# First feed-forward product by Strassen blocks, and the second half of w_out by tokens, in one layer of a hybrid trunk

## The chip, the cores and the metric

One core of a Trainium2 chip. The metric is the device time of one execution in microseconds (us), the median of a few runs. TensorE is called PE, VectorE DVE, ScalarE ACT, GpSimd POOL and SyncE SP; in the code they are `PE` (and `mm` for its matmul), `V`, `S`, `G`, and `dma` is a load that SP issues.

## The reference, cut to what matters

One layer over 640 tokens of 1024 channels: 128 context tokens and 512 latent tokens, which have modulations of their own (shift, scale and gate out of the conditioning). Three mixers work side by side on parts of the channels; then come their output product and a feed-forward net, all in float32.

```python
def trunk_layer(x, mod, ...):
    shift1, scale1, gate1, shift2, scale2, gate2 = jnp.split(mod, 6, axis=-1)
    ...
    mixed = jnp.concatenate([y_a, y_b, y_c], axis=-1)     # 512 + 256 + 256 channels
    x = x + gate1 * jnp.einsum('blc,cd->bld', mixed, w_out)        # 1024 x 1024
    h = rms_norm(x, norm2_g) * (1 + scale2) + shift2
    ff = jnp.square(jax.nn.relu(jnp.einsum('bld,df->blf', h, w_ff1)))   # 1024 x 4096
    x = x + gate2 * jnp.einsum('blf,fd->bld', ff, w_ff2)           # 4096 x 1024
    return x, s_fin
```

A last norm (`final_norm_g`) follows the layer.

## The kernel before

Activations lie channel-major: 128 channels on the partitions, the 640 tokens along the free axis. A float32 product is made of three passes: each operand is split into a high part (`whi`, `fh`, `mh`, made by an ACT cast to fp32r) and a rest (`wlo`, `fl`, `ml`, made by a subtraction on POOL for weights and on DVE for activations), and PE adds high·high, high·rest and rest·high into one bank of PSUM. The 640 tokens are two halves of 320 columns, so that a block of 128 output channels takes 6 matmuls for each 128 input channels. `pm()` hands out the 8 banks of PSUM in turn, all of them named `pb`.

Weights come as 128x512 pieces (`raw`, 256 KB, 2 places) that `wsplit` turns into `whi` and `wlo` (3 places, `WB`). Every engine issues its instructions in a fixed order, written out ahead by a scheduler; an instruction that waits holds up all behind it on its engine.

The mixers and the first half of `w_out` (`out_half`, channels of the FNet and pooling mixers) run in one scheduled stretch that ends at 644.64 us. What follows is what the change touches:

- the second half of `w_out`: the RWKV mixer's output comes back from DRAM (`ycd`, tiles `yc2`), is split into `mh2` and `ml2`, and 8 blocks of 48 matmuls are added, gated, to `x1`. Behind each block ACT and DVE make `h2h` and `h2l`, the parts of `x1` times norm gain and scale but without the norm's division; ACT squares `x1` and POOL adds the squares up (`ssq`).
- the second norm: sums over channels by matmuls with `ones`, mean and epsilon (`st2`) on DVE, the power -0.5 on POOL, a copy along the columns (`rsb`) on DVE, transposes on PE and a copy on ACT give `rs`, the reciprocal root of each token. PE is meanwhile given the first two blocks of the next product (`ahead`), since that uses the operands that are not yet divided.
- the feed-forward net in four quarters of 1024 hidden channels: 8 blocks of the first product (`w_ff1`, 8 x 6 matmuls each; the second half has 2 columns more, which carry the shift), then 8 of the second (`w_ff2`). Behind a block of the first, DVE multiplies by `rs`, ACT adds the shift and takes relu, DVE squares, ACT and DVE split (`fh`, `fl`).
- the last quarter of `w_ff2` runs over 384 tokens and then over 256, with the final norm behind it.

## Time and profile before

| | |
|---|---|
| median of 3 runs (lowest, highest) | 1137.36 us (1137.35, 1138.07) |
| profiled execution | 1140.2 us, which is its span too: nothing of it lies outside |
| PE busy | 1095.3 us (96%) |
| DVE, ACT, POOL busy | 544.5, 506.4, 383.3 us |
| PE's granted clock, mean | 0.983 of full speed |
| chain that ended last | PE 82%, issue 6%, DVE 6%, POOL 2%, ACT 1% |

The three runs lie within 0.07% of each other, and the profiled execution is 2.8 us longer than their median. Times inside the kernel below are from its start. A matmul's busy time is longer than the distance to the next one, since they overlap; what a matmul costs is the distance between starts.

### The profile page before, as it was taken

What the parts mean: (1) busy time and instruction counts of PE and PEld (TensorE: products, weight loads), DVE (VectorE), ACT (ScalarE), POOL (GpSimd) and SP (SyncE); (2) the same over time, 40 slices, a digit from 0 to 9 for tenths busy, and PEclk for the clock granted to TensorE, in tenths of its full rate; (3) what the DMA queues carried; (4) which work ended last, traced back from release to release, by engine and by line L of the source; (5) the groups of instructions that cost most, each with busy time, mean ns of one, the idle gap of its engine ahead of it and who ended that gap; (6) DMA issues with size and microseconds to landing.
All of it is one profiled execution on the core that took longest, in us unless ns stands there. A gap on an engine that the chain in (4) does not pass through costs nothing.

```text
span 1140.2 us, 23679 instructions
## 1 busy us (share of the span) xinstructions
PE 1095.3 (96%) x9516; PEld 949.0 (83%) x9516; DVE 544.5 (48%) x1297; ACT 506.4 (44%) x1221; POOL 383.3 (34%) x462
## 2 busy tenths in 40 slices
PE   5999999999999998998999999999999999999996
PEld 3688888788785665565677999999999999999996
DVE  6266665466665654667754664311331233123313
ACT  5243575655565454654762354312431243124412
POOL 4224431124222133464300283333333333333520
PEclk9999999999998999998999999999999999999999
DMA  9522311111313345442313322222222222222212
GB/s 321 184 62 81 94 36 58 51 51 43 95 64 121 112 139 166 124 133 69 111 56 97 117 74 75 75 75 75 75 76 80 76 76 75 75 74 75 77 45 93
DMA packets 130383, 104.11 MB, mean 91 GB/s; under 512 B 9309, under 2 KB 108642, under 8 KB 130274
## 3 DMA queue, kind: packets, MB, share of 16 engines
q1 hardware_dynamic: 114290, 81.22, 23.5%
q10 hardware_dynamic: 15552, 21.05, 6.2%
q8 instruction: 75, 1.23, 0.4%
q0 software_dynamic: 432, 0.33, 0.2%
q14 instruction: 34, 0.28, 0.1%
HBM read 90.52 MB, written 9.76 MB: 88 GB/s over the span
## 4 chain that ended last, share of the span: by engine, by line
PE 82%; issue 6%; DVE 6%; POOL 2%; ACT 1%; DMA 0%; ACTq 0%; DVEq 0%; POOLq 0%
PE pb L248 82%; DVE t L248 1%; DVE EB L248 1%; DVE bda L248 1%; POOL st L248 1%; DVE P L248 1%; DVE hlo L248 0%; DVE BK L248 0%; POOL t L248 0%; DMA wpl<-w_pool 0%; POOL bda L248 0%; ACTq L248 0%; DVE dd L248 0%; DVE W L248 0%; DVE y L248 0%
## 5 line engine op out<-in xcount | busy, mean ns | idle before, releaser
L248 POOL TENSOR_TENSOR wlo<-raw,whi 128x512 fp32r<-128x512 f32 x125 | 162.3, 1299 | 268.5 <-ACT whi L248 266.2
L248 ACT CAST whi<-raw 128x512 fp32r<-128x512 f32 x161 | 99.8, 620 | 276.6 <-PE pb L248 251.0
L248 PE MATMUL pb<-h2l,whi 128*128 128x320 f32 (+1 forms) x512 | 155.4, 310 | 0.0
L248 PE MATMUL pb<-h2h,whi 128*128 128x320 f32 (+1 forms) x512 | 155.3, 311 | 0.0
L248 DVE SCALAR_TENSOR_TENSOR x<-pb,mod,x 128x128 f32<-128x128 f32 (+1 forms) x144 | 55.0, 433 | 172.9 <-PE pb L248 172.7
L248 PE MATMUL pb<-fh,whi 128*128 128x320 f32 (+2 forms) x408 | 123.3, 310 | 0.0
L248 PE MATMUL pb<-fl,whi 128*128 128x320 f32 (+2 forms) x408 | 122.7, 308 | 0.0
L248 PE MATMUL pb<-h2h,wlo 128*128 128x320 f32 (+1 forms) x512 | 117.0, 310 | 0.0
L248 PE MATMUL pb<-hhi,whi 128*128 128x320 f32 (+1 forms) x304 | 99.1, 331 | 0.0
L248 PE MATMUL pb<-hlo,whi 128*128 128x320 f32 (+1 forms) x304 | 98.6, 329 | 0.4 <-DVE hlo L248 0.4
L248 PEld LDWEIGHTS pb<-h2l,whi 128*128 128x128 f32 x512 | 96.6, 189 | 0.0
L248 PEld LDWEIGHTS pb<-h2h,whi 128*128 128x128 f32 x512 | 96.5, 189 | 0.0
L248 PE MATMUL pb<-fh,wlo 128*128 128x320 f32 (+2 forms) x408 | 94.6, 309 | 0.0
L248 PEld LDWEIGHTS pb<-h2h,wlo 128*128 128x128 f32 x512 | 86.3, 188 | 0.0
L248 POOL TENSOR_TENSOR t<-t,k 128x256 f32<-128x256 f32 (+1 forms) x24 | 15.9, 664 | 208.2 <-DVE t L248 197.5
L248 PE MATMUL pb<-hhi,wlo 128*128 128x320 f32 (+1 forms) x304 | 78.8, 328 | 0.0
L248 PEld LDWEIGHTS pb<-fh,whi 128*128 128x128 f32 x408 | 77.1, 189 | 0.0
L248 PEld LDWEIGHTS pb<-fl,whi 128*128 128x128 f32 x408 | 76.3, 187 | 0.0
L248 DVE TENSOR_TENSOR rl<-pb,rs 128x320 f32<-128x320 f32 x64 | 30.3, 486 | 94.3 <-PE pb L248 94.1
L248 PEld LDWEIGHTS <-bda 128*128 128x128 f16 x880 | 43.1, 99 | 37.8 <-issue 13.9
L248 ACT COPY W<-pb 128x256 f32<-128x256 f32 (+3 forms) x144 | 54.4, 398 | 41.5 <-DVE W L248 29.2
L248 PEld LDWEIGHTS pb<-fh,wlo 128*128 128x128 f32 x408 | 68.6, 188 | 0.0
(271 smaller groups left out, 2399.7 us busy)
## 6 DMA issues: line engine op xcount, KB each, us to landing
raw<-w_ff SPq DMA_DIRECT2D x128, 256.0 KB, 2.8
wa<-w_ada SPq DMA_DIRECT2D x64, 256.0 KB, 3.2
wa<-w_ada SPq DMA_DIRECT2D x16, 512.0 KB, 8.7
raw<-w_in SPq DMA_DIRECT2D x30, 256.0 KB, 2.9
raw<-w_out SPq DMA_DIRECT2D x16, 256.0 KB, 2.8
ukd<-shq ACTq DMA_DIRECT2D x9, 320.0 KB, 2.5
ds<-dft_s ACTq DMA_DIRECT2D x8, 257.0 KB, 2.7
x<-x_sample SPq DMA_DIRECT2D x4, 512.0 KB, 5.8
```

Source lines behind the costliest of these rows:

```text
L248: return fn(out, *a, **k)
```

## The change

The first feed-forward product is done by the Strassen-Winograd scheme on 2 x 2 blocks: two neighbouring blocks of 128 hidden channels (a pair, 16 in all), two halves of the input channels, and two halves of the tokens. Seven products of 4 x 3 matmuls of 320 columns take the place of eight. Four of the seven use sums of weight pieces (`sw`, made on DVE from `rw`, the raw weights of a pair as two loads of 512 KB), and five use sums of activation blocks (`t1` to `t4`, split into `T1` to `T4`; `B11`, `B21`, `B22` are plain blocks). The sums across token halves need operands that are already normalized, so the norm's division, scale and shift are applied to `x1` first (`h2`), and the two extra columns and the multiplication by `rs` behind the product are gone. The products are added up by 7 DVE additions a pair; relu and square are one DVE instruction on 320 columns, followed by the split as before, also on 320.

The second half of `w_out` runs over the first 384 tokens, all 8 blocks, then over the last 256, and each part has sums, root and transposes of its own behind it. The products `w11` and `w12` of the first `LEAD` = 3 pairs need the first half of the tokens alone and are put ahead of the other operands. The place of the final norm's gain and of the first four pieces of the last quarter's weights moves to the end of the feed-forward net.

```diff
-        h2h = fc.tile([P, KB, NT + 2], F32R, name="h2h")
-        h2l = fc.tile([P, KB, NT + 2], F32R, name="h2l")
-        rs = fc.tile([P, NT], F32, name="rs")
+        ba = fc.tile([P, 4 * QW], F32R, name="ba")
+        h2 = fc.tile([P, KB, NT], F32, tag="fh", name="h2")
+        spare = fc.tile([P, KB, NT], F32, tag="fl", name="spare")
...
+        fw = es3.enter_context(tc.tile_pool(name="fw", bufs=1))
+        TOK = ((0, 384), (384, NT))
...
+                r.append(fw.tile([P, 4, 2, P], F32, tag="rw", name="rw", bufs=3))
+                dma(r[-1][:], src[:, 4 * k:4 * k + 4, c0:c0 + 2 * P].rearrange("p k (f c) -> p k f c", f=2))
...
+        def split(w):
+            hi = fw.tile([P, 4, P], F32R, tag="fhi", name="fhi", bufs=6)
+            lo = fw.tile([P, 4, P], F32R, tag="flo", name="flo", bufs=6)
+            S.copy(hi[:], w)
+            G.tensor_tensor(lo[:], w, hi[:].bitcast(F32), op=ALU.subtract)
+            return hi, lo
...
+        def product(w, x):
+            ps = pm()
+            n = 0
+            for kb in range(4):
+                for a, b in ((w[0], x[0]), (w[0], x[1]), (w[1], x[0])):
+                    mm(ps[:, 0:HB], a[:, kb, :], b[:, kb, :], start=n == 0, stop=n == 11)
+                    n += 1
+            return ps[:, 0:HB]
...
+        def lead(w11, w12):
+            p1 = new()
+            S.copy(p1[:], product(w11, B11))
+            c = new()
+            V.tensor_tensor(c[:], p1[:], product(w12, B21), op=ALU.add)
+            return p1, c
...
+                s = fw.tile([P, 4, P], F32, tag="sw", name="sw", bufs=3)
+                V.tensor_tensor(s[:], x, y, op=op)
...
+            s1 = ws(a[1][0], a[1][1], ALU.add)
+            s2 = ws(s1, a[0][0], ALU.subtract)
+            w6 = split(s2)
+            w7 = split(ws(a[0][0], a[1][0], ALU.subtract))
+            w5 = split(s1)
+            w3 = split(ws(a[0][1], s2, ALU.subtract))
+            w4 = split(a[1][1])
...
+            V.tensor_tensor(u2[:], p1[:], product(w6, T2), op=ALU.add)
+            V.tensor_tensor(u3[:], u2[:], product(w7, T3), op=ALU.add)
+            p5 = product(w5, T1)
+            V.tensor_tensor(c22[:], u3[:], p5, op=ALU.add)
+            V.tensor_tensor(u2[:], u2[:], p5, op=ALU.add)
+            emit(1, 1, c22)
+            V.tensor_tensor(u2[:], u2[:], product(w3, B22), op=ALU.add)
+            emit(0, 1, u2)
+            V.tensor_tensor(u3[:], u3[:], product(w4, T4), op=ALU.subtract)
+            emit(1, 0, u3)
...
+                V.scalar_tensor_tensor(c[:], c[:], 0.0, c[:], op0=ALU.max, op1=ALU.mult)
+                last[0] = S.copy(fh[:, b, HALF[h]], c[:]).ins
+                V.tensor_tensor(fl[:, b, HALF[h]], c[:], fh[:, b, HALF[h]].bitcast(F32), op=ALU.subtract)
...
-        with tc.tile_pool(name="mo", bufs=1) as mo:
+        with tc.tile_pool(name="mo", bufs=1, side="right") as mo:
...
+            wo = []
+            for i, (lo, hi) in enumerate(TOK):
+                n = hi - lo
+                for b in range(KB):
+                    if i == 0:
+                        r = wp.tile([P, 4, P], F32, tag="raw", name="raw", bufs=RB)
+                        dma(r[:], w_out[:, 0:4, b * P:(b + 1) * P])
+                        wo.append(wsplit(None, 0, 0, G, r) if b < WB else split(r[:]))
+                    w = wo[b]
...
+                            mm(ps[:, 0:n], x[:, kb, :], y[:, kb, lo:hi], start=m == 0, stop=m == 11)
...
+                        sq = sqs[:, b % 2, :]
+                        S.activation(sq[:, 0:n], x1[:, b, lo:hi], AF.Square)
+                        G.tensor_tensor(ssq[:, lo:hi], ssq[:, lo:hi], sq[:, 0:n], op=ALU.add)
...
+                V.tensor_scalar(st[:, 0:nt], ps[:, 0:nt], 1.0 / D, 1e-6, op0=ALU.mult, op1=ALU.add)
+                G.tensor_tensor(st[:, 3:3 + nt], st[:, 0:nt], half[:, 0:nt], op=ALU.pow)
+                V.tensor_copy(A[:, 0:nt, :], st[:, 3:3 + nt].unsqueeze(2).broadcast_to([P, nt, P]))
...
+                    PE.transpose(ps[:, k * P:(k + 1) * P], A[:, k, :], ident[:])
+                S.copy(rs[:, lo:hi], ps[:, 0:n])
+                cs = HALF[i]
+                for b in range(KB):
+                    V.tensor_tensor(h2[:, b, cs], x1[:, b, cs], rs[:, cs], op=ALU.mult)
+                    for k, ss in ((0, slice(0, NP_)), (1, slice(NP_, HB))) if i == 0 else ((1, cs),):
+                        S.activation(h2[:, b, ss], h2[:, b, ss], AF.Identity, scale=gs2[:, b, k:k + 1], bias=mod[:, 24 + b, k:k + 1])
+                if i == 0:
+                    for k, x in enumerate((B11, B21)):
+                        S.copy(x[0], h2[:, 4 * k:4 * k + 4, cs])
+                        V.tensor_tensor(x[1], h2[:, 4 * k:4 * k + 4, cs], x[0].bitcast(F32), op=ALU.subtract)
...
+        for p in range(LEAD):
+            w11, w12 = wsplit(w_ff1, 2 * p * P, 0, G), wsplit(w_ff1, 2 * p * P, 1, G)
+            first_pairs.append(lead(w11, w12))
...
+        def operand(x, v, eng):
+            S.copy(x[0], v)
+            eng.tensor_tensor(x[1], v, x[0].bitcast(F32), op=ALU.subtract)
+        V.tensor_tensor(t1, b12, b11, op=ALU.subtract)
+        V.tensor_tensor(t2, b22, t1, op=ALU.subtract)
+        operand(T2, t2, V)
+        V.tensor_tensor(t3, b22, b12, op=ALU.subtract)
+        operand(T3, t3, V)
+        operand(T1, t1, G)
+        V.tensor_tensor(t4, t2, b21, op=ALU.subtract)
+        operand(B22, b22, V)
+        operand(T4, t4, V)
...
+        for q in range(4):
+            for p in range(4 * q, 4 * q + 4):
+                r = raw2(w_ff1, 2 * p * P)
+                if p >= LEAD:
+                    first_pairs.append(lead(split(r[0][:, :, 0, :]), split(r[1][:, :, 0, :])))
+                p1, c = first_pairs.pop(0)
+                squares(p)(0, 0, c)
+                rest(p1, r, squares(p))
...
-                pss = gemm(w_out, b * P, (mh, ml), G, (0,))
-                xb = x1[:, b, :]
+                pss = gemm(w_ff2[q], b * P, (fh, fl), G)
                 for h in range(2):
-                    gated(xb, pss[h], h, 2, b, xb)
-                for i, cs in SEG:
-                    S.activation(h2h[:, b, cs], xb[:, cs], AF.Copy, scale=gs2[:, b, i:i + 1])
-                    V.scalar_tensor_tensor(h2l[:, b, cs], xb[:, cs], gs2[:, b, i:i + 1], h2h[:, b, cs].bitcast(F32), op0=ALU.mult, op1=ALU.subtract)
...
-            ahead = [gemm(w_ff1, 0, (h2h, h2l), G, extra=2)]
...
-            ahead.append(gemm(w_ff1, P, (h2h, h2l), G, extra=2))
...
-                    pss = ahead.pop(0) if ahead else gemm(w_ff1, (q * KB + b) * P, (h2h, h2l), G, extra=2)
-                    sb = ffp.tile([P, 2], F32, tag="sb", name="sb", bufs=3)
-                    V.tensor_copy(sb[:], pss[1][:, HB:HB + 2])
...
-                        V.tensor_tensor(t[:, HALF[h]], pss[h][:, 0:HB], rs[:, HALF[h]], op=ALU.mult)
-                    for i, cs in SEG:
-                        S.activation(t[:, cs], t[:, cs], AF.Relu, bias=sb[:, i:i + 1])
-                    V.tensor_tensor(t[:], t[:], t[:], op=ALU.mult)
-                    last = S.copy(fh[:, b, :], t[:]).ins
-                    V.tensor_tensor(fl[:, b, :], t[:], fh[:, b, :].bitcast(F32), op=ALU.subtract)
```

Three places of the static order, before and now. The names are those of the diff; the number behind a name is the tile's.

SP's queue where the RWKV output is loaded back (`yc2`); `raw` are pieces of `w_out` in the second half and the last of the first half. Before:

```order
L248 DMA raw_9330<-w_out 128x4x128 [waits DMAHW3_49,DVE_49]
L248 DMA raw_9427<-w_out 128x4x128 [waits DMAHW4_49,DVE_49]
L248 DMA yc2_9408<-ycd0_157 128x640 [waits DMAHW3_49,DMAHW5_49,PE_49,Pool_49]
L248 DMA yc2_9412<-ycd1_158 128x640 [waits DMAHW6_49]
L248 DMA yc2_9416<-ycd2_159 128x640 [waits DMAHW7_49]
L248 DMA yc2_9420<-ycd3_160 128x640 [waits DMAHW0_49]
L248 DMA raw_9467<-w_out 128x4x128 [waits DMAHW1_49,DMAHW2_49,DVE_49,Activation_49]
```

Now:

```order
L249 DMA raw_9425<-w_out 128x4x128 [waits DMAHW7_49,DMAHW4_49,DVE_49]
L249 DMA rw_9950<-w_ff1 128x4x256 [waits DMAHW6_49,PE_49,Pool_49]
...
L249 DMA raw_9447<-w_out 128x4x128 [waits DMAHW5_49,DVE_49]
L249 DMA raw_9470<-w_out 128x4x128 [waits DMAHW7_49,Pool_49]
L249 DMA rw_10068<-w_ff1 128x4x256
L249 DMA raw_9493<-w_out 128x4x128 [waits DMAHW2_49,Pool_49]
L249 DMA yc2_9409<-ycd0_157 128x640 [waits PE_49]
L249 DMA yc2_9413<-ycd1_158 128x640
L249 DMA yc2_9417<-ycd2_159 128x640 [waits DMAHW0_49]
L249 DMA yc2_9421<-ycd3_160 128x640 [waits DMAHW1_49]
L249 DMA raw_9516<-w_out 128x4x128 [waits DMAHW3_49,Pool_49]
```

Ahead of the four loads of `yc2` now stand three loads of `rw` and three of `raw`; the last two of `raw` wait for POOL.

PE from the second half of `w_out` to the first feed-forward product; `ident` marks the transposes. Before (`mh` and `h2h` are the products around them):

```order
L248 MATMUL pb<-mh_9406,wlo 128x320 x2
L248 MATMUL pb<-h2h,whi 128x320 [waits DMASW0_49,DMASW2_49,DVE_49,Activation_49]
...
L248 MATMUL pb<-h2h,wlo 128x322
L248 MATMUL pb<-ones,ssq 128x1 [waits PE_49,Pool_49]
L248 MATMUL pb<-ones,ssq 128x1 x4
L248 MATMUL pb<-h2h,whi 128x320
...
L248 MATMUL pb<-h2h,wlo 128x322
L248 MATMUL pb<-ident,rsb 128x128 [waits DVE_49]
L248 MATMUL pb<-ident,rsb 128x128 x3
...
L248 MATMUL pb<-h2h,whi 128x320 [waits Activation_49]
```

Now (`spare` holds the sums of squares and the spread-out root, `ba` is `B11` and `B21`):

```order
L249 MATMUL pb<-mh_9407,flo 128x384
L249 MATMUL pb<-ones,spare 128x1 [waits DMASW0_49,DVE_49,DMASW2_49,PE_49,Pool_49]
L249 MATMUL pb<-ones,spare 128x1 x2
L249 MATMUL pb<-ident,spare 128x128 [waits DVE_49,PE_49]
L249 MATMUL pb<-ident,spare 128x128 x2
L249 MATMUL pb<-mh_9407,whi 128x256 [waits PE_49]
...
L249 MATMUL pb<-mh_9407,flo 128x256
L249 MATMUL pb<-ones,spare 128x1 [waits DVE_49,Pool_49]
L249 MATMUL pb<-ones,spare 128x1
L249 MATMUL pb<-ident,spare 128x128 [waits DVE_49]
L249 MATMUL pb<-ident,spare 128x128
L249 MATMUL pb<-ba,whi 128x320 [waits Activation_49]
```

Before, `ones` and the transposes each had a block of `h2h` products ahead of them; now both stand directly behind the products of `w_out` whose tokens they belong to, and the products with 256 columns, or with `ba`, behind them.

POOL around the root of the norm (`st2`, `halfm`): `ssq` and `spare` are the sums of squares, `wlo` and `flo` weight splits. Before:

```order
L248 TENSOR_TENSOR wlo_9794<-raw_9791,whi_9793 128x512 [waits DMAHW1_49,PE_49,Activation_49]
L248 TENSOR_TENSOR ssq_9424<-ssq_9424,sq_9714 128x640 [waits Activation_49,Pool_49]
L248 TENSOR_TENSOR wlo_9835<-raw_9832,whi_9834 128x512 [waits DMAHW2_49,PE_49,Activation_49]
L248 TENSOR_TENSOR ssq_9424<-ssq_9424,sq_9756 128x640 [waits Activation_49,Pool_49]
L248 TENSOR_TENSOR wlo_9865<-raw_9862,whi_9864 128x512 [waits DMAHW3_49,PE_49,Activation_49]
L248 TENSOR_TENSOR st2_9827<-st2_9827,halfm_87 128x5 [waits DVE_49]
L248 TENSOR_TENSOR wlo_9934<-raw_9931,whi_9933 128x512 [waits DMAHW4_49,PE_49,Activation_49]
```

Now, for the last 256 tokens:

```order
L249 TENSOR_TENSOR spare_9398<-spare_9398 128x256 [waits Activation_49]
L249 TENSOR_TENSOR spare_9398<-spare_9398 128x256 [waits Activation_49,Pool_49]
L249 TENSOR_TENSOR wlo_9811<-raw_9808,whi_9810 128x512 [waits DMAHW7_49,PE_49,Activation_49]
L249 TENSOR_TENSOR spare_9398<-spare_9398 128x256 [waits Activation_49,Pool_49] x2
L249 TENSOR_TENSOR wlo_9817<-raw_9814,whi_9816 128x512 [waits DMAHW0_49,PE_49,Activation_49]
L249 TENSOR_TENSOR spare_9398<-spare_9398 128x256 [waits Activation_49,Pool_49] x2
L249 TENSOR_TENSOR flo_9968<-sw_9965,fhi_9967 128x512 [waits PE_49,Activation_49]
L249 TENSOR_TENSOR spare_9398<-spare_9398 128x256 [waits Activation_49,Pool_49]
L249 TENSOR_TENSOR flo_9972<-sw_9957,fhi_9971 128x512 [waits PE_49,Activation_49]
L249 TENSOR_TENSOR st2_9779<-st2_9779,halfm_87 128x2 [waits DVE_49]
```

Seven additions of 256 columns stand there, with four splits of the first pair's weights among them and the root behind.

## Rows read from the trace of the kernel before

**Rows 1.** The page's first lines: span, and busy time of each engine.

```profile
span 1140.2 us, 23679 instructions
...
PE 1095.3 (96%) x9516; PEld 949.0 (83%) x9516; DVE 544.5 (48%) x1297; ACT 506.4 (44%) x1221; POOL 383.3 (34%) x462
```

**Rows 2.** The chain that ended last, in order of time: start us, us, what.

```profile
628.13 503.34 PE pb L248 x3414
```

**Rows 3.** Windows: us, busy us (count) of PE, PEld, DVE, ACT, POOL; PEclk; DMA.

```profile
900.00:1000.00 100.00, 100.00 (x680) 100.00 (x680) 27.67 (x59) 32.33 (x53) 36.18 (x28) 1.00 0.26 75
```

**Rows 4.** Groups by form, 700 to 1040 us: count, busy us, mean ns.

```profile
L248 POOL TENSOR_TENSOR wlo<-raw,whi 128x512 fp32r<-128x512 f32 x97 | 125.3, 1292 | 217.8 <-ACT whi L248 217.8
...
L248 DVE TENSOR_TENSOR rl<-pb,rs 128x320 f32<-128x320 f32 x48 | 22.9, 486 | 79.1 <-PE pb L248 79.1
L248 DVE TENSOR_TENSOR fl<-rl,fh 128x640 fp32r<-128x640 f32 x25 | 20.6, 826 | 19.8 <-ACT fh L248 19.8
...
L248 ACT ACTIVATE rl<-rl,sb 128x512 f32<-128x512 f32 x24 | 17.4, 725 | 0.0
L248 DVE SCALAR_TENSOR_TENSOR x<-pb,mod,x 128x320 f32<-128x320 f32 x24 | 13.0, 542 | 0.0
...
L248 ACT ACTIVATE rl<-rl,sb 128x128 f32<-128x128 f32 x24 | 9.7, 404 | 1.8
```

**Rows 5.** The window of the second half of w_out, columns as in rows 3.

```profile
644.64:672.80 28.16, 28.16 (x194) 28.16 (x193) 22.64 (x40) 17.87 (x32) 21.87 (x15) 1.00 0.27 77
```

**Rows 6.** Timeline of PE in the tail: start us, us, instruction.

```profile
1076.06 0.34 PE L248 MATMUL pb<-fh,whi 128*128 128x384 f32 x1
...
1076.58 0.34 PE L248 MATMUL pb<-fh,h2h 128*128 128x384 f32 x1
...
1118.27 0.28 PE L248 MATMUL pb<-fh,h2l 128*128 128x256 f32 x1
...
1118.63 0.28 PE L248 MATMUL pb<-fh,h2l 128*128 128x256 f32 x1
```

**Rows 7.** Timeline of SP's queue.

```profile
624.32 12.17 SPq L248 DMA_DIRECT2D raw<-w_out  x2
636.65 2.81 SPq L248 DMA_DIRECT2D yc<-ycd  x4
```

**Rows 8.** Timeline of ACT.

```profile
640.65 0.73 ACT L248 CAST mh<-yc 128x640 fp32r<-128x640 f32 x1 [0.56 <-DMA yc<-ycd]
...
644.54 0.73 ACT L248 CAST mh<-yc 128x640 fp32r<-128x640 f32 x1 [0.16 <-DMA yc<-ycd]
```

**Rows 9.** Timeline of DVE.

```profile
681.14 0.17 DVE L248 TENSOR_SCALAR st<-pb 128x5 f32<-128x5 f32 x1 [5.17 <-PE pb L248]
682.59 0.82 DVE L248 COPY rsb<-st 128x640 f32<-128x640 f32 x1 [1.29 <-POOL st L248]
...
693.88 1.53 DVE L248 TENSOR_TENSOR fl<-rl,fh 128x640 fp32r<-128x640 f32 x1 [0.31 <-ACT fh L248]
```

**Rows 10.** Timeline of POOL.

```profile
655.68 1.57 POOL L248 TENSOR_TENSOR ssq<-ssq,sq 128x640 f32<-128x640 f32 x1 [1.26 <-ACT sq L248]
...
658.52 2.03 POOL L248 TENSOR_TENSOR ssq<-ssq,sq 128x640 f32<-128x640 f32 x1
...
681.38 1.18 POOL L248 TENSOR_TENSOR st<-st,halfm 128x5 f32<-128x5 f32 x1 [2.74 <-DVE st L248]
...
693.30 1.43 POOL L248 TENSOR_TENSOR wlo<-raw,whi 128x512 fp32r<-128x512 f32 x1 [3.19 <-ACT whi L248]
```

**Rows 11.** Group by form on DVE, 644 to 682 us.

```profile
L248 DVE SCALAR_TENSOR_TENSOR h2l<-x,gs,h2h 128x512 fp32r<-128x512 f32 x8 | 8.6, 1076 | 1.6 <-ACT h2h L248 1.6
```

**Rows 12.** Windows before the second half of w_out, columns as in rows 3.

```profile
626.00:631.00 5.00, 3.06 (x9) 2.07 (x9) 1.50 (x3) 0.00 (x0) 1.46 (x1) 0.50 0.30 75
...
632.00:634.00 2.00, 2.00 (x13) 1.65 (x12) 1.86 (x5) 0.00 (x0) 0.00 (x0) 1.00 0.00 0
```

More of the change, by code (lines that the diff above doesn't have):

```diff
@@ L103 @@
 RS = 1024.0
+LEAD = 3
 ENGS = (mybir.EngineType.PE, mybir.EngineType.DVE, mybir.EngineType.Activation, mybir.EngineType.Pool)
@@ L1608, in build @@
-                if b == 0:
-                    S.activation(ssq[:], xb, AF.Square)
-                else:
-                    sq = mo.tile([P, NT], F32, tag="sq", name="sq", bufs=2)
-                    S.activation(sq[:], xb, AF.Square)
-                    G.tensor_tensor(ssq[:], ssq[:], sq[:], op=ALU.add)
-            ahead = [gemm(w_ff1, 0, (h2h, h2l), G, extra=2)]
-            ps = pm()
-            for t in range(5):
-                mm(ps[:, t:t + 1], ssq[:, t * P:(t + 1) * P], ones[:], start=True, stop=True)
```

219 lines of the change are left out of this document (121 added, 98 removed).

## The prediction

> **What bounds the kernel now.** I read the page's first lines, then the chain, then windows along the stretch that changes. PE is busy for 1095.3 of 1140.2 us [rows 1], and the chain's last link is one run of 3414 matmul pieces from 628.13 us to 1131.5, without a stall [rows 2]. In a window of the feed-forward net PE is busy for 100 of 100 us at full clock, POOL for 36, ACT for 32 and DVE for 28 [rows 3]. So two things count: how much PE work goes, and whether PE still finds its operands. The second has no slack to draw on: at present nothing waits, so each new wait of PE is added to the span.
>
> **What is removed.** 680 matmuls take 100 us, 0.147 us each [rows 3]. The first product had 4 quarters x 8 blocks x 8 input blocks x 6 = 1536; 16 pairs x 7 products x 12 make 1344. The 192 removed are worth 28.2 us, and the two extra columns on 768 matmuls another 768 x 0.147 x 2/320 = 0.7. Together -28.9 us.
>
> The second half of w_out takes 28.16 us [rows 5]. In the tail three matmuls of 384 columns take 0.52 us, three of 256 take 0.36 [rows 6], so 96 of each come to 16.6 + 11.5 = 28.1: no change.
>
> **What is added ahead of the feed-forward net.** The order puts four stops of PE there, which nothing on PE can pass, and a slower clock behind them.
>
> 1. *The loads of yc2.* Before, they went out at 636.65, behind two raw loads [rows 7]; the first cast began 4.0 us later, the last 7.9 [rows 8], while PE had out_half to do until 644.64 [rows 5]. Now six loads stand ahead, and the last raw waits for POOL's split of the raw two before it, whose whi needs a place that PE frees with the last block but one, 24 x 0.147 = 3.5 us before 644.64, at 641.1. A wait for that raw's landing of about 1 us, a cast of 0.7 and a split of 1.3 [rows 4] later it is 644. The loads then go out at about 645, since they stand behind one more issue, the last cast begins at 653, and block 0, whose matmuls need all four pieces, ends at about 655 instead of 647. I take 8 us; at the least 1 (mh2 lies where out_half's operands were, so its cast waits for PE's last matmul in any case), at the most 10.
>
> 2. *The root for 384 tokens.* ones and transposes stand directly behind the products. After the last matmul come an evacuation (0.8, by 0.54 for 320 columns [rows 4], now in two pieces), a square (0.6, between 0.40 for 128 and 0.73 for 512 [rows 4]), POOL's addition (1.0, from 1.57 for 640 [rows 10]), ones 0.3, st2 0.17 [rows 9], the power (0.9, from 1.18 for five columns [rows 10]), the spread (0.6, from 0.82 for 640 [rows 9]), the transposes 0.4, and handoffs. 5.5 us, between 4 and 6.5. Before, this chain lay behind the blocks of `ahead`.
>
> 3. *The root for 256 tokens.* Its bare chain is about 4 us, but the engines come to it late. The 256 pass takes 11.5 us on PE. ACT first does rs (0.6), sixteen activations (8 x 0.72) and two casts of 1280 (2.7): 9 to 10 us before its first square of this pass. Only then can POOL do its seven additions (0.75 each) and, among and behind them, four splits of 1.29 [rows 4]: 10.4 us. So ones comes at about 19 us and, since DVE's row ahead of st2 waits for the fourth split, the transposes at about 22.5. That is 11 us behind the pass; between 7 and 13.
>
> 4. *The operand T2.* The leads hide 72 x 0.147 = 10.6 us. In this time DVE does h2 (8 x 0.45), t1, t2, t3, t4 and T2's rest (1.4 each for 1280 columns, by 0.83 for 640 [rows 4]), and T2's rest comes at 12 to 14 us. 2.5 us; between 0 and 5.
>
> 5. *The clock.* At 626 to 631 us, after a stop and thin work, PE was granted 0.50, its lower level (1.2 of 2.4 GHz), and did 3.1 us of work at it, half of which the full clock would have saved; from 632 it was back at 1.00 [rows 12]. The stops 1 to 3 are longer than that one. Three times 1.5 us is 4.5; between 0 and 7.5.
>
> Sum 8 + 5.5 + 11 + 2.5 + 4.5 = 31.5 us, with ends at 12 and 42.
>
> **What is added in the feed-forward net.** A pair takes PE 84 x 0.147 = 12.3 us. POOL has 7 splits, 9.0 us. DVE has 7 additions out of PSUM (0.486 each), 4 sums of weights (0.69 each, by 0.83 for 640) and 8 instructions of 320 (0.45): 9.8 us [rows 4]. Alone, each fits. Together they cost more: an ssq took 2.03 us beside DVE's h2l and 1.57 elsewhere [rows 10], and the h2l of 512 columns took 1.08 on average [rows 11] where 0.69 would be in proportion. DVE has 4608 columns of such two-input work a pair, 7.2 times the 640 of one h2l; 7.2 x 0.46 = 3.3 brings POOL to 12.3, and 9 x 0.39 = 3.5 brings DVE to 13.3. That is just PE's own time. The splits run up to six products ahead (six places of fhi), the eight banks let PE run ahead of DVE, and 5.3 us of w_ff2 pass before the last blocks of fh are read, so the later quarters lose little. The first loses most: three of its pairs have 60 matmuls only (8.8 us), while DVE still makes T3, B22 and T4. I take 3 us for the whole net; nothing at the least, and 22 at the most (below).
>
> The other edits I cost at nothing: w_ff1's bytes are the same and the DMA engines are a quarter busy [rows 3]; ACT's seven casts of 512, one copy and four casts of 320 are about 7 us a pair (0.7 and 0.55 each [rows 4]) and fit into 12.3, and if they didn't the splits would come late by the difference; the last quarter's tail is the same work.
>
> **The sum.** 1140.2 - 28.9 + 31.5 + 3 = 1145.8 in the profiled execution's own time. The runs' median is 2.8 below that execution, so 1143.0, 0.5% slower. 0.2% (2.3 us) is about what a measurement can tell from no change. The gain decides against the stops: with the net's 3 us, it is faster below 24 us of stops in all, and slower above 28.
>
> **The rivals.**
>
> *Loads in time (faster).* If SP isn't held by the waits ahead, the loads of yc2 land before out_half ends. Stop 1 falls from 8 to 1 and takes its 1.5 us of clock with it: 1143.0 - 8.5 = 1134.5, 0.25% faster. For it: before, the same loads went out at 636.65 [rows 7]. Against it: then two loads of 256 KB stood ahead, and it took 12.2 us until both were issued [rows 7]; now six do. It decides when the last yc2 lands before about 647; a landing before about 649.5, with all else as above, gives no change.
>
> *The second root is hidden better (no change).* If ACT does its squares at PE's pace, with the activations for h2 spread between them, stop 3 is its bare chain of 4 us: 1143.0 - 7 = 1136.0, 0.1% below the median. For it: POOL has nothing to do for much of the pass (seven additions of 0.75 fit into 11.5 us). Against it: four splits stand between and behind the additions, and the places of three of them come free only as the pass proceeds.
>
> *The shared port (slower).* One of POOL and DVE stands still whenever the other has a two-input instruction. Then 9.0 + 4 x 0.69 + 8 x 0.45 = 15.4 us a pair stand against PE's 12.3: 3.1 x 4 = 12.3 a quarter, less six splits of head start (7.7), is 4.6 in each of three quarters, and about 8 in the first, whose operands use the port as well. 22 us instead of 3: 1162. For it: a fl that began 0.58 us after a wlo ended 0.68 after the wlo's end and took 1.53 [rows 9, 10], where 0.83 is usual [rows 4]. Against it: the ssq that lost 0.46 us beside an h2l whose own length is about 0.69, so that the two ran side by side for a part [rows 10, 11]. It decides when the two engines' instructions add up to more than PE's 12.3 a pair.
>
> The Trainium skill ("SBUF — State Buffer", section "SBUF: two separate sides") states this last as the rule: the port pair that VectorE and GpSimd share is an exclusive lock, held for a whole instruction, and a VectorE instruction with two SBUF inputs needs it against a GpSimd instruction that reads SBUF. By that rule the time would be that rival's 1162; the trace agrees in the fl (1.53 us), and not in the ssq (0.46 us lost, not 0.69).
>
> **How the numbers follow.** The forecast, with stops of 28 to 38 us: 0.37, slower; the same sum with 24 to 28: 0.03, no change. Loads in time: 0.14, faster. The second root hidden: 0.12, half of it faster, half no change. Both together, 1127.5 and, with the clock undisturbed, 1122: 0.14, faster. The port: 0.15, slower. Something else, such as a split that waits for a sum of weights on DVE, or gaps that are all at their low ends: 0.05, 0.03 of it faster. That is 0.37 faster, 0.09 no change, 0.54 slower. The range reaches from the two rivals together to the port, 1122 to 1161; that of the forecast alone is 1139 to 1151.
>
> **What would show it.** The products of the first net must start 0.147 us apart in each pair; if they don't, the 28.9 is wrong. Stops of PE before the first `ba` product show 1, 2, 3 as idle of 8, 5 and 11 us, released by yc2's casts and by the transposes' operands; the clock row should read 0.5 behind each. T2 shows as an idle before the first product with `bt`. The net is right if each quarter's first product takes 49.3 us of PE with little idle; wlo and flo splits near 1.3 us speak against the port, 1.9 and DVE's two-input rows near twice their length for it. I am wrong if the loads of yc2 go out before 640 us, or if PE idles between the pairs of the later quarters.

## The result, and the profile of the changed kernel

The changed kernel takes 1204.17 us (median of 4 runs, 1197.08 to 1206.25); the kernel before took 1137.36 us (4 runs, 1135.61 to 1138.07). The ratio is 1.0563, 95% interval [1.0515, 1.0611]: 5.6% slower. The direction was the one with the highest chance in the prediction (0.54 for slower); the size lies 43 us above the end of its range.

The page's first lines, with the row of the granted clock in 40 slices, answer to [rows 1]:

```profile
span 1204.4 us, 23667 instructions
...
PE 1098.5 (91%) x9316; PEld 944.3 (78%) x9324; DVE 686.3 (57%) x1452; ACT 516.8 (43%) x1275; POOL 464.4 (39%) x519
...
PEclk9999999999999999999897878889998999999999
```

There are 200 matmul records fewer, but PE is busy for longer, since part of the work ran at the lower clock. In [rows 2] the chain ended with one run of 3414 matmul pieces. Now that stretch of the chain is broken by work of DVE, ACT and POOL. Windows of the stretches of the change (columns as in [rows 3]) show where:

```profile
674.55:680.52 5.97, 1.51 (x11) 1.30 (x10) 1.46 (x4) 0.52 (x1) 2.44 (x3) 0.84 0.00 0
680.52:694.25 13.73, 13.73 (x98) 13.71 (x96) 8.29 (x16) 11.36 (x24) 2.51 (x2) 0.82 0.00 0
694.25:707.48 13.23, 1.55 (x9) 1.27 (x7) 6.30 (x8) 4.85 (x10) 13.07 (x13) 0.68 0.14 40
707.48:729.88 22.40, 16.99 (x75) 16.02 (x74) 20.55 (x18) 14.09 (x21) 13.74 (x7) 0.73 0.31 95
729.88:778.60 48.72, 43.73 (x267) 43.21 (x267) 43.34 (x59) 16.81 (x33) 29.21 (x20) 0.90 0.24 71
...
790.27:906.57 116.30, 109.13 (x720) 107.59 (x720) 62.49 (x101) 33.91 (x64) 59.50 (x44) 0.97 0.25 73
```

The rows are: the root for 384 tokens, the pass over 256 tokens, its root, the leads (the `w11` and `w12` products of the first three pairs), the rest of the first quarter's pairs, and a round. A round is a second product and the next first product, 720 matmuls. Where PE runs through one without a stop it takes 105.6 us (e1, e8): this one is 10.7 us too long, and the next, to 1022.75, 10.6. The leads have 72, 10.6 us, and take 22.4. The four pairs of the first quarter have 264 left, 38.8 us, and take 48.7.

PE's timeline names what it stood for (start us, us, instruction, idle before and what ended it):

```profile
652.65 0.69 PE L249 MATMUL pb<-mh,whi 128*128 128x384 f32 x1 [5.83 <-ACT mh L249]
...
677.29 0.83 PE L249 MATMUL pb<-ones,spare 128*128 128x1 f32 x6 [2.59 <-POOL spare L249]
679.99 0.87 PE L249 MATMUL pb<-ident,spare 128*128 128x128 f32 x3 [1.87 <-DVE spare L249]
...
702.96 1.01 PE L249 MATMUL pb<-ones,spare 128*128 128x1 f32 x4 [8.52 <-POOL spare L249]
707.14 0.69 PE L249 MATMUL pb<-ident,spare 128*128 128x128 f32 x2 [3.17 <-DVE spare L249]
...
717.33 0.93 PE L249 MATMUL pb<-ba,whi 128*128 128x320 f32 x3 [1.94 <-ACT whi L249]
...
727.05 0.64 PE L249 MATMUL pb<-ba,wlo 128*128 128x320 f32 x1 [2.57 <-POOL wlo L249]
...
905.66 0.64 PE L249 MATMUL pb<-fh,whi 128*128 128x320 f32 x1 [6.04 <-ACT fh L249]
...
1138.65 0.44 PE L249 MATMUL pb<-fh,ba 128*128 128x384 f32 x1 [4.50 <-ACT ba L249]
1140.00 0.69 PE L249 MATMUL pb<-fh,ba 128*128 128x384 f32 x1 [0.90 <-POOL ba L249]
```

The first five rows are stops 1 to 3 of the prediction, at their places (stops 2 and 3 are two waits each, one ahead of `ones` and one ahead of the transposes). The next two lie in the leads, and wait for weight splits, not for T2. The wait of 6.04 us stands at the start of a second product: the last blocks of `fh` are late, because the whole first product fell behind. The last two are a load in the tail that the prediction didn't have.

Inside the net, groups by form from 852 to 906 us (count, busy us, mean ns, idle before) answer to [rows 4]:

```profile
L249 POOL TENSOR_TENSOR flo<-sw,fhi 128x512 fp32r<-128x512 f32 x16 | 22.9, 1447 | 5.5 <-ACT fhi L249 4.1 <-PE pb L249 1.3
...
L249 DVE SCALAR_TENSOR_TENSOR us<-us 128x320 f32<-128x320 f32 x14 | 19.4, 1388 | 0.1
...
L249 DVE TENSOR_TENSOR us<-us,pb 128x320 f32<-128x320 f32 x25 | 11.7, 481 | 1.7 <-PE pb L249 1.1
...
L249 ACT CAST fh<-us 128x320 fp32r<-128x320 f32 x14 | 6.5, 462 | 27.0 <-DVE us L249 27.0
```

Relu and square (`us<-us`) takes 1.39 us on average; with POOL's splits gone the same instruction takes 0.49 (experiment e1). The additions with one operand in PSUM stay at 0.48. ACT stands 27.0 us of these 54 for that one DVE instruction. How the wait goes round shows in the timelines of POOL, DVE and ACT:

```profile
875.37 1.46 POOL L249 TENSOR_TENSOR flo<-rw,fhi 128x512 fp32r<-128x512 f32 x1 [1.45 <-ACT fhi L249]
878.27 1.29 POOL L249 TENSOR_TENSOR flo<-rw,fhi 128x512 fp32r<-128x512 f32 x1 [1.45 <-ACT fhi L249]
...
875.60 1.58 DVE L249 SCALAR_TENSOR_TENSOR us<-us 128x320 f32<-128x320 f32 x1
...
877.21 0.46 ACT L249 CAST fh<-us 128x320 fp32r<-128x320 f32 x1 [1.60 <-DVE us L249]
877.58 0.62 ACT L249 CAST fhi<-rw 128x512 fp32r<-128x512 f32 x1
```

POOL's split runs from 875.37 to 876.83. DVE's relu-square begins at 875.60 and ends at 877.18, 0.35 after the split. ACT's cast of `fh` waits for it, and the cast `fhi` of the next split stands behind that one in ACT's order. So POOL's next split begins at 878.27, after 1.45 us of idleness, and the next relu-square meets it. In the chain that ended last the run of PE is followed by such links, and the same two splits of each pair stand 15.48 us apart, where PE needs 12.3 for a pair. Over two pairs (866.78 to 897.71) POOL is busy for 19.6 of 30.9 us and DVE for 27.0, so neither is full by itself:

```profile
790.27 61.87 PE pb L249 x405
...
866.78 2.80 POOL flo L249 x2
...
882.26 2.80 POOL flo L249 x2
```

### The profile page after: what moved, and what is told of

The parts are those of the page before. It is cut to its first block, busy times and chain, and to the rows that moved or that the text cites. A ratio compares the mean times of both kernels' runs of the same rounds, so it can differ in the third digit from the quotient of the medians.

```text
span 1204.4 us, 23667 instructions
## 1 busy us (share of the span) xinstructions
PE 1098.5 (91%) x9316; PEld 944.3 (78%) x9324; DVE 686.3 (57%) x1452; ACT 516.8 (43%) x1275; POOL 464.4 (39%) x519
## 4 chain that ended last, share of the span: by engine, by line
PE 62%; DVE 15%; issue 12%; POOL 6%; DMA 3%; ACT 2%; SPq 0%; ACTq 0%; POOLq 0%; DVEq 0%
PE pb L249 62%; DVE us L249 5%; POOL flo L249 3%; DVE sw L249 3%; DVE fl L249 2%; DVE t L249 1%; POOL wlo L249 1%; DVE EB L249 1%; DMA raw<-w_ff 1%; POOL st L249 1%; DVE bda L249 1%; DMA x<-x_sample 1%; ACT fh L249 1%; DVE P L249 0%; DMA yc<-ycd 0%
## 5 line engine op out<-in xcount | busy, mean ns | idle before, releaser
L249 PE MATMUL pb<-bt,fhi 128*128 128x320 f32 x640 | 144.9, 315 | 3.8 <-ACT fhi L249 3.7
L249 POOL TENSOR_TENSOR wlo<-raw,whi 128x512 fp32r<-128x512 f32 x62 | 85.5, 1381 | 133.2 <-ACT whi L249 133.2
L249 ACT CAST whi<-raw 128x512 fp32r<-128x512 f32 x98 | 60.4, 619 | 170.6 <-PE pb L249 151.5
L249 PEld LDWEIGHTS pb<-bt,fhi 128*128 128x128 f32 x640 | 110.3, 193 | 4.4 <-ACT fhi L249 4.4
L249 POOL TENSOR_TENSOR flo<-sw,fhi 128x512 fp32r<-128x512 f32 x64 | 91.6, 1445 | 34.3 <-ACT fhi L249 30.3
L249 PE MATMUL pb<-bt,flo 128*128 128x320 f32 x320 | 101.3, 316 | 3.7 <-POOL flo L249 3.7
L249 POOL TENSOR_TENSOR t<-t,k 128x256 f32<-128x256 f32 (+1 forms) x24 | 16.2, 673 | 206.4 <-DVE t L249 195.7
L249 DVE SCALAR_TENSOR_TENSOR us<-us 128x320 f32<-128x320 f32 x64 | 76.3, 1194 | 0.6
L249 POOL TENSOR_TENSOR flo<-rw,fhi 128x512 fp32r<-128x512 f32 x42 | 57.5, 1371 | 48.1 <-ACT fhi L249 28.8
L249 ACT CAST fh<-us 128x320 fp32r<-128x320 f32 x64 | 29.4, 461 | 106.8 <-DVE us L249 106.8
L249 POOL TENSOR_TENSOR st<-st,halfm 128x1 f32<-128x1 f32 (+3 forms) x20 | 25.0, 1252 | 129.4 <-DVE st L249 129.4
```

What stands on the lines that cost most here:

```text
L249: return fn(out, *a, **k)
```

## The experiments

The theory after the result: the net is held by POOL's weight splits and DVE's two-operand work getting in each other's way, and by ACT's order, which carries the delay back to POOL. Rivals: DVE has simply too much to do; the scarce places for sums of weights (`sw`) hold it. For the part ahead of the net, each stop has its own cause. e1 to e8 are one profiled execution each, compared with the changed kernel's 1204.4 us; e9 to e12 were timed.

The spans of single executions are good to several us only: the changed kernel's own four runs lie 9.2 us apart, and PE comes to the end of out_half, ahead of what the edits are about, anywhere between 640.4 and 649.2 us. Two other times don't depend on that: from PE's last matmul of out_half to the end, and a round, from the first product with `fh` in the second quarter to the first in the third. Out of PE's timelines, in us:

| run | span | end of out_half | from there to the end | a round |
|---|---|---|---|---|
| changed kernel | 1204.4 | 646.8 | 557.6 | 116.2 |
| e1 | 1160.0 | 648.2 | 511.8 | 105.6 |
| e2 | 1183.2 | 644.1 | 539.1 | 111.9 |
| e3 | 1193.0 | 643.7 | 549.3 | 115.9 |
| e4 | 1198.5 | 645.2 | 553.3 | 116.3 |
| e5 | 1204.3 | 642.3 | 562.0 | 120.6 |
| e6 | 1200.5 | 649.2 | 551.3 | 117.2 |
| e8 | 1161.8 | 640.4 | 521.4 | 105.6 |

**e1: no splits on POOL in the net.** The low parts of the first feed-forward weights, but for the six pieces of the leads, are replaced by a tile of zeros, so this kernel leaves out the products with the rests of those weights; PE does the same number of matmuls.

```diff
...
-            lo = fw.tile([P, 4, P], F32R, tag="flo", name="flo", bufs=6)
             S.copy(hi[:], w)
+            if ff:
+                return hi, zlo
...
```

> The changed kernel without POOL's splits of the weights in the first feed-forward product (the low parts are a tile of zeros there, so the rest of the weights is left out of that product; the matmuls are as many). If DVE and POOL shut each other out (9.0 + 6.4 = 15.4 us a pair), the relu-squares on DVE fall from 1.2 to about 0.5 us, a pair is bound by PE (12.3 us), the stop of 6 us ahead of each second product goes, and the whole falls from 1204 to about 1165. If DVE is too slow by itself, in its own order, the stops stay and the whole stays above 1190.

Span 1160.0. The chain ends with one long run, and the relu-square on DVE (second fence: groups by form, 800 to 1040 us) is back at its own length:

```profile
726.05 359.35 PE pb L249 x2433
```

```profile
L249 DVE SCALAR_TENSOR_TENSOR us<-us 128x320 f32<-128x320 f32 x32 | 15.6, 487 | 0.3
```

With POOL quiet, DVE does all its own work of the net without holding PE: a round takes 105.6 us, which is PE's own time. DVE's load alone is not the cause; of the span 44 us go with POOL's splits, 46 behind the end of out_half. The waits in the leads remain.

**e2: relu and square on ACT.**

```diff
-                V.scalar_tensor_tensor(c[:], c[:], 0.0, c[:], op0=ALU.max, op1=ALU.mult)
+                S.activation(c[:], c[:], AF.Relu)
+                S.activation(c[:], c[:], AF.Square)
```

> Relu and square go from DVE (one instruction of two SBUF inputs) to ACT (two instructions, 3.7 us a pair more on ACT, which has about 7 of 12.3). POOL's work is the same. Shared port: DVE and POOL then need 9.0 + 2.8 + 1.8 = 13.6 us a pair, 54.4 a quarter, less 7.7 of head start, which is under PE's 49.3: the stops ahead of the second products nearly go, about 1175. If POOL's own pace were the bound, the stops stay at 6 us and the time at 1200 or more, since POOL has no less to do.

Span 1183.2, 8 above what was expected; a round takes 111.9 us. The stop ahead of a second product shrinks from 6.04 to 2.39 us and doesn't go away:

```profile
890.05 0.63 PE L249 MATMUL pb<-fh,whi 128*128 128x320 f32 x1 [2.39 <-ACT fh L249]
```

POOL has as many splits as before, so POOL's own pace alone is not what sets a round. Taking the squares off DVE helps, so they are a part of it; the sums of weights still meet the splits (one of a pair's four sums, `sw<-rw,sw`, took 1.61 us on average here and 0.69 in e1).

**e5 and e6: five places for the sums of weights in place of three,** in the changed kernel and in e2.

```diff
-                s = fw.tile([P, 4, P], F32, tag="sw", name="sw", bufs=3)
+                s = fw.tile([P, 4, P], F32, tag="sw", name="sw", bufs=5)
```

> The changed kernel with five places for the sums of weights in place of three. If the period of 15.45 us a pair is the sum of what POOL and DVE do one after the other (9.0 + 6.4), it stays within 0.3 us of that and the whole within 5 us of 1204. If it is a loop (a sum waits for the place that POOL's split gives back, ACT's cast waits for the sum, POOL's next split for the cast), two more places break it: 13.5 us or less a pair, and about 1180.

> Relu and square on ACT, and five places for the sums of weights. One after the other: 9.0 + 2.8 + 1.8 = 13.6 us a pair as with three places (13.68), the whole within 4 us of 1183. The loop over three places: the pair falls to PE's 12.3 us, the stops ahead of the second products go, and the whole is about 1168.

e5: the span of 1204.3 is as expected, but by luck. The first quarter ended sooner, and the later rounds took 2.8 to 4.7 us longer. A pair was to stay at 15.45 us; the same split of POOL in two pairs lies 17.2 us apart, and the next one 16.2 behind it (at 999.97):

```profile
966.59 1.46 POOL L249 TENSOR_TENSOR flo<-sw,fhi 128x512 fp32r<-128x512 f32 x1 [2.84 <-ACT fhi L249]
983.78 1.46 POOL L249 TENSOR_TENSOR flo<-sw,fhi 128x512 fp32r<-128x512 f32 x1 [2.84 <-ACT fhi L249]
```

More places don't free the net; they slow its pairs. e6: 1200.5, where 1183 or 1168 was expected. More room made e2 slower, by 17 us of span, 12 behind the end of out_half, and a pair takes 15.5 us where e2 has 13.7. Both theories missed e5's pair and e6. Its waits from 852 to 906 us (total, times, longest) show POOL idle for ACT's casts and DVE for raw weights:

```profile
POOL flo L249 <- ACT fhi L249: 14.5, 9, 3.7
DVE sw L249 <- DMA rw<-w_ff: 7.0, 2, 3.6
```

My reading, which no run tests by itself: with more places DVE makes its sums earlier, meets other splits, and then waits for raw weights, which have three places. What the runs do show is that the period of a pair is not a plain sum of POOL's and DVE's times. The sum fits the changed kernel (15.4 for 15.5) and e2 (13.6 for 13.7), and misses e5 (15.4 for 16.2 to 17.2) and e6 (13.6 for 15.5).

**e7: the two engines measured by themselves.** Trains of the same shapes, two times over, alone and side by side; nothing of the layer is computed.

> Not the layer (nothing of the reference is computed): short trains of the same instructions, alone and side by side, twice over. Alone: 8 POOL subtractions of 512 take 10.3 us, 24 DVE subtractions of 512 about 14.6, 24 additions out of PSUM 9.7, 12 relu-squares and 12 additions in turn 9.7. Exclusion: POOL's 8 beside 24 subtractions take 25 us together, beside 24 additions out of PSUM 10.3, beside the train in turn about 15.3 with relu-squares of 1.3 us each. Sharing: beside the subtractions both end within about 18 us, each instruction longer by a part. ACT's squares of 320 stay at 0.46 us beside POOL in both.

Timelines of POOL and DVE (8 splits alone; beside 24 two-operand instructions; beside 24 additions out of PSUM; then DVE's trains in the same places, and one relu-square that met a split):

```profile
5.96 10.64 POOL L300 TENSOR_TENSOR g<-w,hi 128x512 f32<-128x512 f32 x8
...
39.77 13.44 POOL L300 TENSOR_TENSOR g<-w,hi 128x512 f32<-128x512 f32 x8 [0.51 <-DVE a L296]
65.69 10.68 POOL L300 TENSOR_TENSOR g<-w,hi 128x512 f32<-128x512 f32 x8 [0.51 <-DVE a L296]
...
17.53 5.78 DVE L304 TENSOR_TENSOR c<-a,w 128x512 f32<-128x512 f32 x8
...
39.73 24.93 DVE L304 TENSOR_TENSOR c<-a,w 128x512 f32<-128x512 f32 x24
65.65 12.48 DVE L312 TENSOR_TENSOR c<-a,ps 128x320 f32<-128x320 f32 x24
...
80.17 0.92 DVE L308 SCALAR_TENSOR_TENSOR c<-a 128x320 f32<-128x320 f32 x1
```

24 two-operand instructions alone would take 3 x 5.78 = 17.3 us; beside 8 splits they took 24.93, and POOL 13.44. Both were as expected of exclusion (25 us), and not of sharing (18). While POOL's train ran, 8 splits and 8 such instructions passed in 13.44 us, 3.0 less than in turn (10.64 + 5.78 = 16.4), 0.37 a pair of instructions. For each split DVE stood still for 0.95 us (7.6 by 8), and POOL for 0.35 (2.8 by 8). An operand in PSUM lifts it entirely (12.48 us for 24, 4.13 for 8 alone, and POOL 10.68), and beside 24 squares on ACT POOL took 10.67. In the train in turn a relu-square that met a split took 0.92 us, where 1.3 was expected of exclusion. It began 1.0 us into a split and ended 0.35 us behind it (that split ran from 79.17 to 80.74); in the kernel the relu-square of 1.58 us began 0.23 us into its split and also ended 0.35 behind it. The Trainium skill ("SBUF — State Buffer", section "SBUF: two separate sides") calls the port pair that VectorE and GpSimd share an exclusive lock; e7 agrees but for these 0.37 us.

**e8: the splits on DVE.** Then the two engines have nothing to exclude each other for.

```diff
-            G.tensor_tensor(lo[:], w, hi[:].bitcast(F32), op=ALU.subtract)
+            V.tensor_tensor(lo[:], w, hi[:].bitcast(F32), op=ALU.subtract)
```

> The splits of the first feed-forward product subtract on DVE in place of POOL, so that POOL is out of that stage and DVE has 9.8 + 7 x 0.69 = 14.6 us a pair, all at its own pace. Exclusion: 14.6 in place of 15.45 a pair, relu-squares of 0.5 us, about 3 us less a quarter and the whole at 1185 to 1195. If DVE is slow by itself (13.3 us a pair or more without POOL's work), the pair takes 18 and the whole is above 1230.

Span 1161.8, far better than the 1185 to 1195 expected; of the 42.6 us gained 6.4 lie ahead of the end of out_half, and 36.2 behind it. A round takes 105.6 us. The chain's long run, and groups by form from 790 to 900 us:

```profile
760.85 325.59 PE pb L249 x2218
```

```profile
L249 DVE TENSOR_TENSOR flo<-sw,fhi 128x512 fp32r<-128x512 f32 x16 | 10.9, 686 | 0.0
...
L249 DVE SCALAR_TENSOR_TENSOR us<-us 128x320 f32<-128x320 f32 x16 | 7.7, 483 | 0.0
```

A split takes 0.69 us on DVE, 1.29 to 1.45 on POOL, and the three later quarters run without a stop. DVE alone carries more than before and is quicker than DVE and POOL together. The expectation priced DVE too high: instructions overlap at their ends, and in the changed kernel an `sw` of 0.68 us that began at 874.59 was followed at 875.20, the `fl` of 0.48 there at 875.60. By starts a pair is 11 x 0.61 + 15 x 0.40 = 12.7 us on DVE, an estimate, hardly more than PE's 12.3, and the second product makes it up.

**e3: a place of their own for the loads of `yc2`** (that of `h2`, not yet in use).

```diff
-                yc = mo.tile([P, NT], F32, tag="yc", name="yc2", bufs=4)
-                dma(yc[:], ycd[kb][:])
+                yc = h2[:, kb, :]
+                dma(yc, ycd[kb][:])
```

> The RWKV output is loaded into the free place of h2 in place of a tile of its own behind out_half's operands; in SP's order its four loads then stand ahead of the weights of the first product. If the stop of 5.8 us and the half clock behind it came from the late loads, the 384 pass begins within 2 us of out_half's end and the whole falls by 8 to 10 us, to about 1195. If the weights of w_out, now behind, take its place, it stays within 3 us of 1204.

Span 1193.0, as expected; behind the end of out_half the gain is 8.3 of these 11.4 us. Of 5.83 us of stop 1 are left:

```profile
645.10 0.62 PE L249 MATMUL pb<-mh,whi 128*128 128x384 f32 x2 [1.39 <-ACT mh L249]
```

**e4: 384 and 256 columns block by block, both roots behind.**

```diff
-            for i, (lo, hi) in enumerate(TOK):
-                n = hi - lo
-                for b in range(KB):
+            for b in range(KB):
+                for i, (lo, hi) in enumerate(TOK):
+                    n = hi - lo
```

> The token split is undone in time alone: each block of w_out does 384 and then 256 columns, and both roots come behind the last block. If the two stops of the norm (8.2 and 15.6 us with their clock) are each a chain that nothing covers, one stop of about 16 us (one chain, then h2, B11 and B21 in the open) takes their place: about 1197. If what counts is the length of the queues on ACT, DVE and POOL, which is the same work in a shorter time, the leads come no earlier than now, and the whole is at 1204 or above.

Span 1198.5, as expected, but not for the reason given. The two stops of the norm have become one stop and a wait for B11's cast, and the leads begin no sooner: 61.6 us behind the end of out_half (at 706.83), where the changed kernel has 60.7 (at 707.48). The second theory said that, and 1204 or more. The time was won behind it: from the first lead to the first second product it took 65.7 us in place of 70.7. PE's waits from 640 to 735 us:

```profile
PE pb L249 <- POOL spare L249: 9.4, 1, 9.4
PE pb L249 <- ACT ba L249: 8.7, 2, 8.2
```

**e9 to e11: the mends together.** e9 is e3, e4 and e8. e10 is e9 with the sums of squares on DVE and B11's cast directly behind its own four blocks of `h2`; e11 is e10 with the leads' splits on DVE.

```diff
-                        G.tensor_tensor(ssq[:, lo:hi], ssq[:, lo:hi], sq[:, 0:n], op=ALU.add)
+                        V.tensor_tensor(ssq[:, lo:hi], ssq[:, lo:hi], sq[:, 0:n], op=ALU.add)
...
-            w11, w12 = wsplit(w_ff1, 2 * p * P, 0, G), wsplit(w_ff1, 2 * p * P, 1, G)
+            w11, w12 = wsplit(w_ff1, 2 * p * P, 0, V), wsplit(w_ff1, 2 * p * P, 1, V)
```

> Three edits at once: the first product's splits on DVE, the RWKV output into the place of h2, and both column passes of w_out block by block. If the stops add up one by one, 1162 - 11 - 6 = 1145 us, within 4 us. If the shorter way to the norm only brings the first pairs up against the splits and sums on DVE sooner, 1152 or more.

> As the one before, and the sums of squares on DVE in place of POOL, and B11 cast as soon as its four blocks of h2 are there. If POOL's queue of additions was what made ones late (the 9.4 us before ones with the blocks' order), that stop falls to 3 to 4 us, and B11 comes 3 us sooner: about 1136. If the chain is as long on DVE, since it has the evacuations too: 1143 or more.

> As the one before, and the splits of the six lead products on DVE too, so that POOL subtracts nothing but T1's rest between the root and the second product. With POOL they take up to 2.5 us each beside DVE's sums, and hold DVE up as well: 3 us less than the one before. If DVE's own queue is what the leads and T2 wait for, it is 2 us more.

Medians 1154.99, 1156.33 and 1154.55 us; ratios to the kernel before 1.0134 [1.0089, 1.0179], 1.0157 [1.0108, 1.0205] and 1.0128 [1.0088, 1.0167]. e9 missed its 1145 and e10 its 1136; both came out as their rivals had it (1152 or more, 1143 or more). e11 was to be 3 us below e10; between the three no difference can be told. In e9 PE waited 8.2 us in one piece for B11 and 6.4 for the sums; in e10 5.3 for B11, 4.0 ahead of `ones` and 4.5 in one piece for a lead's split. Each mend moved the wait to the next of these; the chain from the last product to B11 stayed.

**e12: two of the tail's pieces loaded early,** into places of their own, otherwise e11.

```diff
+                    order_after(dma(er[k][:], w_ff2[3][:, kb:kb + 4, b * P:(b + 1) * P]).ins, last[0])
...
+                            raw = er[n - WB] if n < WB + 2 else op.tile([P, 4, P], F32, tag="raw", name="raw", bufs=4)
```

> As e11, but the first two of the late pieces of the last quarter's w_ff2 have a place of their own and are loaded before the last quarter, where e11 loads them behind the final norm's gain into memory that comes free with the feed-forward net's own tiles. In the changed kernel PE waits 4.50 us for the cast of the first such piece and 0.90 for its rest (1138.65 and 1140.00 us), in the versions without stalls in the net 2.3 and 0.9. Theory, that the late load is the cause: both waits together fall from 3.2 to 1 us at most, and the median from 1154.6 to about 1152. Rival, that the cast is late because it stands behind the last fh cast on ACT: the waits stay at 2 us or more with the load long landed, and the median stays within 1 us of 1154.6.

Median 1147.13 us, ratio 1.0083 [1.0050, 1.0115]: the best version found, still 0.8% slower than the kernel before. The wait in the tail is gone, and from the first quarter to the tail's end PE runs in one piece. The median fell by 7.4 us, where 2.6 was expected. The chain, then PE's waits from 640 to 745 us, then a window:

```profile
734.10 401.31 PE pb L249 x2727
```

```profile
PE pb L249 <- ACT ba L249: 5.3, 1, 5.3
PE pb L249 <- ACT fhi L249: 4.5, 1, 4.5
```

```profile
640.29:734.10 93.81, 69.50 (x400) 66.42 (x400) 80.95 (x141) 49.76 (x92) 13.58 (x8) 0.85 0.28 84
```

Before, the run from the end of out_half to the end of the tail's products took 486.8 us, from 644.64 to 1131.5 [rows 2, 5]. With the saving of 30.3 (next section) it would be 456.5; here it is 495.1, from 640.29 to 1135.41. The 38.6 us of losses lie ahead of 734.10: 24.3 of waits (nine groups, of 3.5 us or less, not shown), and 14.3 of which the most is the clock, 0.85 in the mean of that stretch. 38.6 less 30.3 is 8.3; the median is 8.6 above that of the kernel before in the same comparison (1138.53). e12's profiled span is 11.2 us below e11's: 6.2 of that lie ahead of the second half of w_out, which e12 doesn't touch (PE's first product of the second half of w_out starts at 641.99 against 648.17), and 5.0 in the net and the tail, where e11's wait of 3.1 and the clock behind it stood. The ratios' intervals overlap, so that e12 is better than e11 rests on the wait that is gone more than on the medians.

## Why the prediction was wrong

The profiled execution is 64.2 us longer than that of before. The saving can be read from stretches that PE does in one piece: the first product of the second quarter before, and that of the third in e12 (windows, columns as in [rows 3]).

```profile
787.68:844.53 56.85, 56.85 (x387) 56.85 (x385) 19.38 (x38) 22.90 (x38) 20.67 (x16) 1.00 0.27 75
```

```profile
919.75:969.03 49.28, 49.28 (x338) 49.28 (x337) 46.01 (x95) 22.33 (x44) 1.30 (x1) 1.00 0.28 85
```

That is 7.57 us a quarter, 30.3 in all. With it there are 94.5 us of losses; the prediction had 34.5 (31.5 and 3). The losses are a stretch's length less its matmuls' time.

| step of the prediction | predicted us | measured us |
|---|---|---|
| what is removed | -28.9 | -30.3 (4 x 7.57) |
| stops 1 to 3 with their clock | 29.0 | 32.9 (34.0 for 16.6 of work, 27.0 for 11.5) |
| 4, the operand T2 (the leads) | 2.5 | 11.8 (22.4 for 10.6) |
| the net: first quarter and 40 matmuls of its second product | 3 for the whole net | 15.7 (60.4 for 304 matmuls) |
| the net: two rounds | | 21.3 (232.5 for 2 x 105.6) |
| the net: last quarter and tail | "the same work" | 10.9, by difference |
| ahead of the change | 0 | 1.9 (the window of the change begins at 646.50, before at 644.64) |

**The saving held, and stops 1 to 3 in their sum.** The saving is 1.4 us larger, since the two extra columns cost 0.53 us a quarter (56.85 less the 56.32 of a second product, which has as many matmuls without them) and not 0.7 in all. Stop 1: the loads of `yc2` were issued at 648.45 (predicted about 645), behind the raw that waits for POOL, as SP's queue shows:

```profile
648.03 0.37 SPq L249 DMA_DIRECT2D raw<-w_out  x1
648.45 1.92 SPq L249 DMA_DIRECT2D yc<-ycd  x4
```

Stop 1 with its clock cost 11.4 us, for 9.5 predicted, but its wait was shorter (6.2 for 8) and the clock behind it dearer (5.2 for 1.5): that the sum is near is luck in part. Stop 2 took 6.0 and the half clock behind it 2.2, for 7; stop 3 13.2, for 11, released by POOL's sums and DVE's spread root as forecast. With the 2.5 us behind stop 3, which lie in the leads, the clock's term was 9.9 us, where the prediction had 4.5 and at most 7.5. e3 takes stop 1 away at about its price.

**Step 4 failed in size and in cause.** "The operand T2. 2.5 us" looked for the wait at T2. PE stood inside the leads instead: 1.94 us for a weight cast that is queued behind the eight activations of `h2` on ACT, 2.57 for a lead's rest on POOL that stood behind T1's rest (2.97 us) and took 2.51 us while DVE made the operands (a free one takes 1.29), 0.90 for another. These are 5.4 us. The other 6.4 are the lower clock: up to 712.40, and again behind the leads' own short waits (0.53 from 719.42 to 722.97, 0.50 from 727.05). I had counted DVE's work there and not what ACT's and POOL's orders put ahead of the leads' weights, nor a slower clock behind waits of 2 us.

**The net failed: "I take 3 us for the whole net".** The step was the estimate of how POOL and DVE share. I let 0.46 us per meeting for POOL and 0.39 per 512 columns for DVE, from an ssq that ran partly beside an h2l [rows 10, 11], stand for all two-operand work, and set the fl of 1.53 us [rows 9], which lost 0.70, aside for it. In e7 DVE loses 0.95 us to a split of 512 columns, and in the net a relu-square of 320 loses 0.90 (1.39 against 0.49): 3.6 us a pair for these four alone, where 3.5 was allowed for all of DVE. And I let both engines' delays run side by side (12.3 and 13.3, "just PE's own time"), where ACT's order chains one to the other: 15.5 us a pair.

The rival "the shared port" had the right mechanism. That its 15.4 us a pair lies so near the 15.5 measured is luck in part, since the same sum misses e5 and e6. Its 22 us was too low as well: it forecast 4.6 us for a round, and a round had 7.1 us of waits (6.0, 0.8 and 0.3) and a slower clock behind them (0.53 from 906.57 to 911.00, which costs 2.1). The first quarter lost 15.7, 10.7 of it in waits, where the rival had 8. e1 and e8 show by opposite means that POOL's splits beside DVE are the cause: without them there, a round is PE's own 105.6 us. That ACT's order adds to it is seen in the timelines, but how much of the 3.2 us a pair the order alone makes was not separated.

**"The last quarter's tail is the same work" failed.** The same work starts later: its first loads wait for memory that the net's own tiles hold (`gf` goes out at 1132.59, the first raw at 1132.98, behind the last rest of `fh`), and PE stood 4.50 and 0.90 us for them. From its first product to its last the tail took 68.3 us, where before it took 59.7. The order showed the move, and I priced it at nothing without naming the cover. In e8, where the net no longer stalls, the tail still takes 66.0 us; in e12, where the first two loads come early, 59.9.

**The break-even held.** With the net mended (e12) the losses ahead of it are 38.6 us and the gain is 30.3: slower, as the prediction had it for more than 28 us of stops. That this is near its 28 to 38 us is luck, since e12 also mends stop 1 and reorders the rest. Two ends of the range don't follow from its terms: with 3.0 us of clock left, 1127.5 becomes 1124.5 and not 1122, and the port rival's 1162 stands as 1161. Neither bears on the outcome. Not tried: leaving the first quarter in its old form, whose products would hide the norm.
